# Three reorderings in a fused two-layer transformer trunk: ties on weight splits and residual additions, gate and up products grouped by half, and a split last output tile

## The chip, the cores and the metric

The kernel runs on one core of one Trainium2 chip. The metric is the device time of one execution in microseconds (us), lower is better. TensorE (PE; its weight loads are PEld) multiplies, VectorE (DVE) and ScalarE (ACT) do the elementwise work, GpSimd (POOL) a few small operations, and the queue of SyncE (SP) issues nearly all transfers.

## The reference

A trunk of two pre-norm layers on a residual stream x of 256 tokens by 1024 features, in float32:

```
for layer in (0, 1):
    h = rmsnorm(x, norm_mix[layer])
    x = x + mixer[layer](h @ w_in) @ w_out        # even: indexed sparse + differential attention; odd: compressed + selected + window attention
    h = rmsnorm(x, norm_ffn[layer])
    x = x + (silu(h @ w_gate) * (h @ w_up)) @ w_down      # 2816 hidden features
return rmsnorm(x, norm_final)
```

## The kernel before, in words

Tokens lie in two tiles t = 0, 1 of 128. Every float32 product of an activation with a weight is made of three in a reduced format: each operand is split into a high part (a rounding copy on ACT) and a low part (the difference, on DVE), and high x high, high x low and low x high are added up in PSUM. In the gate and up products (L438, L439) the activation's high and low parts lie side by side, so that one product of 512 columns takes both against the weight's high part, and a second of 256 columns adds the weight's low part.

Weights stream through the class `Weights` as 200 tiles of up to 128 x 1024, in the order of use: per layer the input projection, eight tiles of the output projection, 44 of gate and up, 22 of the down projection. `load` issues a transfer on SP's queue (four raw buffers), `prepare` makes the high part (L110, ACT) and the low part (L113, DVE; seven buffers of each), and `next` hands a tile out and prepares up to six ahead. With `hold=tail` the last tiles of an output or down projection are handed out together.

`residual` multiplies out a projection for the four quarters (t, h), h being a half of 512 features. It runs k by k over all quarters, and for the last `tail` k quarter by quarter, so that one quarter ends early: its sum is added to x (L382 or L384) and the next norm's work on it begins (`Norm.half`: weighting by the gain, four transposes, the split into `aW`; or `Final.half` for the output). In the mixers the order is (0,0), the first half of (0,1), (1,0), the rest of (0,1), (1,1). `amid` is called after the first entry; in the even mixer it transposes and splits the attention output of tile 1.

The softmax of the odd mixer (`softmax_terms`, L401 on DVE and L402 on ACT) runs for two groups gp, each for t = 0, 1; then the terms are scaled (L917, DVE), transposed (L922), copied out (L218) and multiplied by the values (L938).

The program is written in order, but a planner lists each engine's instructions: among those that are ready by its own clock it takes the one of the highest priority, which follows program order. A NoSync tie fixes only the order of two instructions in the list of one engine; `keep_in_program_order` (`pin`) ties an instruction behind all that was traced before it on its engine. Each engine then works through its list in order.

Of the kernel before, what the change touches and what calls it, by code (L numbers as in the profile page):

```python
# [55 lines left out]
C_SEL = C_CMP + NT * 16  # L56
C_BM = C_SEL + 2 * P
C_KM = C_BM + 8
C_END = C_KM + 2

# [14 lines left out]
class Weights:  # L75


    def __init__(self, tc, pool, rpool, flats, specs, ahead, bufs, spare):
# [9 lines left out]
        self.ready = []  # L88
        self.used = 0

# [7 lines left out]
    def prepare(self, upto, behind=False):  # L98

        nc = self.tc.nc  # L100
        while len(self.ready) < min(upto, len(self.queue)):
# [8 lines left out]
            act = nc.scalar.activation(hi[:, :n], raw[:, :n], AF.Copy)  # L110
            if behind:
                self.tc.keep_in_program_order(act)
            nc.vector.tensor_sub(lo[:, :n], raw[:, :n], hi[:, :n])  # L113
# [11 lines left out]
def trunk(tc, x, w0, w1, sm0, cw, vec, gcol, cst, out, dbg=None):  # L125
# [91 lines left out]
    def evac(dst, src):  # L217
        A.activation(dst, src, AF.Copy)  # L218
# [21 lines left out]

    def split(hi, lo, src):
        A.activation(hi, src, AF.Copy)
        V.tensor_sub(lo, src, hi)  # L243

    def split_T(dst, k0, src, n, behind=False):

        pt = t_bank("pt_a").rearrange("p (k c) -> p k c", k=4)
        for i in range(n):
            mmi = TE.transpose(pt[:, i], src[:, i * P : (i + 1) * P], ident)
            if behind:  # L250
                pin(mmi)
        split(dst[0][:, k0 : k0 + n], dst[1][:, k0 : k0 + n], pt[:, :n])

    class Norm:


        def __init__(self, goff):
            self.goff = goff
            self.wide, self.aT = new_wide()
            self.rs = [small_tile(1, "rs") for _ in range(NT)]  # L260
            self.last = None
            self.ms = [None] * NT

        def finish(self):

            if self.last is not None:
                split_T(self.aT[NT - 1], 4, self.last, 4, behind=True)
                self.last = None

        def half(self, t, h):  # L270
# [5 lines left out]
            else:  # L276
                split_T(self.aT[t], 4 * h, xg, 4)
# [28 lines left out]
    class Final:  # L306


        def __init__(self):
            self.ms = [small_tile(2, "ms2") for _ in range(NT)]  # L310
            self.y = [[nat("y") for _ in range(2)] for _ in range(NT)]

        def half(self, t, h):
            ms = self.ms[t]
            c = slice(512 * h, 512 * h + 512)
            sq = ap.tile([P, 512], BF16, tag="sq", bufs=2, name="sq")
            A.activation(sq, xs[t][:, c], AF.Square, scale=1.0 / math.sqrt(D), accum_out=ms[:, h : h + 1])
            V.tensor_mul(self.y[t][h], xs[t][:, c], gains[V_FIN][:, c])
            if h == 1:
                rf = small_tile(1, "ms")  # L320
                rsqrt_sum(rf, ms)
                for h in range(2):
                    c = slice(512 * h, 512 * h + 512)
                    y = self.y[t][h]
                    if h == 0:
                        A.activation(y, y, AF.Copy, scale=rf)
                    else:
                        V.tensor_scalar(y, y, rf, None, op0=ALU.mult)
                    (A, nc.sync)[h].dma_start(out[t * P : (t + 1) * P, c], y)

    def mm3(ps, act, k, wh, wl, start, stop):
        TE.matmul(ps, act[0][:, k], wh, start=start, stop=False)  # L332
        TE.matmul(ps, act[0][:, k], wl, start=False, stop=False)  # L333
        TE.matmul(ps, act[1][:, k], wh, start=False, stop=stop)  # L334
# [15 lines left out]
    def residual(act, nk, tail, nxt, rs=None, amid=None):  # L350

        ps = [[mm_bank("ps_out") for _ in range(2)] for _ in range(NT)]

        def one(t, h, k, wt):
            c = slice(512 * h, 512 * h + 512)
            mm3(ps[t][h], act[t], k, wt[0][:, 0, c], wt[1][:, 0, c], k == 0, k == nk - 1)
# [7 lines left out]
        if amid:  # L364
# [5 lines left out]
        for t, h, k0, k1 in order:  # L370
            c = slice(512 * h, 512 * h + 512)
            for k in range(k0, k1):
                one(t, h, nk - tail + k, last[k])
# [7 lines left out]
            if rs is None:  # L381
                V.tensor_add(xs[t][:, c], ps[t][h], xs[t][:, c])  # L382
# [706 lines left out]
```

## Time and profile before

| what | value |
|---|---|
| time, median of 3 runs | 656.94 us (656.31 to 657.65) |
| the profiled execution | 658.92 us, of which the span of its trace is 657.1 us |
| PE / DVE / ACT / POOL busy | 98% / 74% / 60% / 2% of the span |
| granted clock of PE | full speed (2.4 GHz level) nearly throughout; mean 0.997 |
| read from HBM | 107.46 MB, 165 GB/s over the span |

Starts and durations in the rows below are us from the start of the span, means are ns. Matmuls overlap and their ends are modelled: the pace is read from start to start. "[0.70 <-DVE xg L273]" is idle time of the engine just before the instruction, and what ended it.

The stages by time: even mixer to 138, its gate and up to 263, down projection to 325, odd mixer to 467, its gate and up to 590, down projection to 650, then the end of the final norm and the store.

### The profile page before, as it was taken

Reading aid. Unit: us, or ns where it says so; the run is one execution under the profiler, and the core shown is the slowest. Engines: PE = TensorE matmul, PEld = TensorE weight load, DVE = VectorE, ACT = ScalarE, POOL = GpSimd, SP = SyncE. Lnnn points to the kernel's source line nnn. Section 1 sums busy time; section 2 is a strip of 40 time slices with the busy share of each in tenths; the row PEclk is TensorE's granted clock in tenths of the full one; section 3 lists DMA queues with packets and bytes.
Section 4 is the critical chain, followed back from the end, with each engine's and each line's share of the span. In section 5 each row is a group of like instructions: output and inputs, shape, how many; then the busy total and the mean of one; then the engine's idle time right before and its main releaser. Section 6 shows DMA issues by size and latency. Waiting matters only on the chain.

```text
span 657.1 us, 10010 instructions
## 1 busy us (share of the span) xinstructions
PE 643.1 (98%) x3512; PEld 537.5 (82%) x3512; DVE 489.0 (74%) x1115; ACT 395.7 (60%) x800; POOL 12.9 (2%) x26
## 2 busy tenths in 40 slices
PE   8999999999999999999999999999999999999995
PEld 5979888788888888888887877776888888888884
DVE  6999977778877777544588888796788787875424
ACT  6686758557655555433476698696586555554312
POOL 2000000000000000000000000000000000000000
PEclk9999999999999999999999999999999999999998
DMA  8834354418765665664187331412176555555501
GB/s 309 305 118 145 97 189 134 126 35 290 237 182 188 192 185 181 190 196 143 49 342 268 105 95 64 161 33 97 67 262 247 189 188 192 182 191 192 193 23 65
DMA packets 31729, 109.15 MB, mean 166 GB/s; under 512 B 3648, under 2 KB 3904, under 8 KB 31424
## 3 DMA queue, kind: packets, MB, share of 16 engines
q1 hardware_dynamic: 31104, 107.92, 49.2%
q10 hardware_dynamic: 576, 0.59, 0.3%
q8 instruction: 28, 0.46, 0.3%
q14 instruction: 21, 0.17, 0.1%
HBM read 107.46 MB, written 1.05 MB: 165 GB/s over the span
## 4 chain that ended last, share of the span: by engine, by line
PE 84%; DVE 8%; ACT 3%; issue 2%; DMA 1%; POOL 0%; SPq 0%; POOLq 0%; DVEq 0%; ACTq 0%
PE ps_g L438 12%; PE ps_u L438 12%; PE ps_out L332 7%; PE ps_out L334 7%; PE ps_out L333 7%; PE ps_g L439 6%; PE ps_u L439 6%; PE ps_in L333 4%; PE ps_in L332 4%; PE ps_in L334 4%; DVE w_lo L113 3%; PE ps_o L938 2%; PE ps_s L903 2%; PE pt_p L922 1%; PE ps_s L624 1%
## 5 line engine op out<-in xcount | busy, mean ns | idle before, releaser
L113 DVE TENSOR_TENSOR w_lo<-w_raw,w_hi 128x1024 fp32r<-128x1024 f32 (+5 forms) x200 | 234.7, 1180 | 90.1 <-ACT w_hi L110 87.3
L110 ACT ACTIVATE w_hi<-w_raw 128x1024 fp32r<-128x1024 f32 (+5 forms) x200 | 203.0, 1023 | 127.5 <-PE ps_out L334 56.8
L438 PE MATMUL ps_g<-aW,w_hi 128*128 128x512 f32 x352 | 124.5, 396 | 0.3 <-DVE aW L243 0.3
L438 PE MATMUL ps_u<-aW,w_hi 128*128 128x512 f32 x352 | 124.4, 395 | 0.0
L439 PE MATMUL ps_g<-aW,w_lo 128*128 128x256 f32 x352 | 98.7, 280 | 0.0
L439 PE MATMUL ps_u<-aW,w_lo 128*128 128x256 f32 x352 | 98.7, 280 | 0.0
L438 PEld LDWEIGHTS ps_g<-aW,w_hi 128*128 128x128 f32 x352 | 66.0, 187 | 16.4 <-DVE aW L243 0.9
L438 PEld LDWEIGHTS ps_u<-aW,w_hi 128*128 128x128 f32 x352 | 66.0, 187 | 15.4
L333 PE MATMUL ps_in<-w_lo,aW 128*128 128x512 f32 (+5 forms) x208 | 76.9, 370 | 0.1
L332 PE MATMUL ps_in<-w_hi,aW 128*128 128x512 f32 (+5 forms) x208 | 76.7, 369 | 0.1
L334 PE MATMUL ps_in<-w_hi,aW 128*128 128x512 f32 (+5 forms) x208 | 75.8, 365 | 0.0
L333 PE MATMUL ps_out<-w_lo,hT_hi 128*128 128x512 f32 x176 | 68.6, 390 | 0.0
L334 PE MATMUL ps_out<-w_hi,hT_lo 128*128 128x512 f32 x176 | 68.6, 390 | 0.0
L332 PE MATMUL ps_out<-w_hi,hT_hi 128*128 128x512 f32 x176 | 68.6, 390 | 0.0
L439 PEld LDWEIGHTS ps_g<-aW,w_lo 128*128 128x128 f32 x352 | 66.5, 189 | 0.0
L439 PEld LDWEIGHTS ps_u<-aW,w_lo 128*128 128x128 f32 x352 | 66.5, 189 | 0.0
L333 PEld LDWEIGHTS ps_in<-w_lo,aW 128*128 128x128 f32 x208 | 39.3, 189 | 4.7 <-issue 0.5
L332 PEld LDWEIGHTS ps_in<-w_hi,aW 128*128 128x128 f32 x208 | 39.2, 189 | 4.8 <-ACT w_hi L110 0.3
L334 PEld LDWEIGHTS ps_in<-w_hi,aW 128*128 128x128 f32 x208 | 39.3, 189 | 4.6 <-issue 0.5
L402 ACT ACTIVATE e<-e,bias 128x128 f32<-128x128 f32 (+1 forms) x96 | 42.4, 445 | 0.9 <-DVE bias L401 0.9
L334 PEld LDWEIGHTS ps_out<-w_hi,hT_lo 128*128 128x128 f32 x176 | 33.0, 188 | 6.8
L333 PEld LDWEIGHTS ps_out<-w_lo,hT_hi 128*128 128x128 f32 x176 | 33.0, 188 | 6.8
(225 smaller groups left out, 888.1 us busy)
## 6 DMA issues: line engine op xcount, KB each, us to landing
w_raw<-in_w SPq DMA_DIRECT2D x176, 512.0 KB, 4.3
w_raw<-in_w SPq DMA_DIRECT2D x8, 384.0 KB, 4.6
gain<-in_vec SPq DMA_DIRECT2D x4, 512.0 KB, 5.4
cw<-in_cw SPq DMA_DIRECT2D x2, 1024.0 KB, 8.5
w_raw<-in_w SPq DMA_DIRECT2D x4, 416.0 KB, 5.6
w_raw<-in_w SPq DMA_DIRECT2D x4, 328.0 KB, 5.2
w_raw<-in_w SPq DMA_DIRECT2D x4, 304.0 KB, 2.9
x<-in_x SPq DMA_DIRECT2D x4, 256.0 KB, 5.2
```

The lines of the kernel that those rows point to most:

```text
L110: act = nc.scalar.activation(hi[:, :n], raw[:, :n], AF.Copy)
L113: nc.vector.tensor_sub(lo[:, :n], raw[:, :n], hi[:, :n])
L332: TE.matmul(ps, act[0][:, k], wh, start=start, stop=False)
L333: TE.matmul(ps, act[0][:, k], wl, start=False, stop=False)
L334: TE.matmul(ps, act[1][:, k], wh, start=False, stop=stop)
L402: A.activation(e, e, AF.Exp, scale=-1.0, bias=bias, accum_out=den)
L438: TE.matmul(dst[f], wh[:, i, c], wide[:, k].rearrange("p z q -> p (z q)"), start=k == 0, stop=False)
L439: TE.matmul(dst[f][:, :T], wl[:, i, c], wide[:, k, 0], start=False, stop=k == KD - 1)
L624: TE.matmul(sb[:, i], qT[:96, h0 + i, tq], kT[:96, h0 + i, :ns], start=True, stop=True)
L903: mmi = TE.matmul(sb[:, i], qS[t][:, h], kz[:, par, :, :ns], start=z == 0, stop=z == 1)
L922: TE.transpose(pt[:, i, b, st], e[:, i, b, st * P : (st + 1) * P], ident)
L938: pin(TE.matmul(ob[64 * par : 64 * par + 64], vv[:, st, c : c + 64], pTs[par][:, b, st].rearrange("p j c -> p (j c)"), start=False, stop=l ...
```

## The change

The diff, cut to its core. `behind(ins, other)` adds a NoSync tie.

```diff
 Weights.prepare:
+            with self.tc.high_priority(offset=-self.later):
                 act = nc.scalar.activation(hi[:, :n], raw[:, :n], AF.Copy)
...
+                sub = nc.vector.tensor_sub(lo[:, :n], raw[:, :n], hi[:, :n])
+                self.parts.append((act, sub))
 Final:
+        def square(self, t, o, n, last=False):
+            i = self.part[t]
+            self.part[t] += 1
+            ms, total = self.ms[t], self.sum[t]
+            sq = ap.tile([P, 512], BF16, tag="sq", bufs=2, name="sq")
+            pin(A.activation(sq[:, :n], xs[t][:, o : o + n], AF.Square, scale=1.0 / math.sqrt(D), accum_out=ms[:, i : i + 1]))
+            if not last:
+                pin(A.activation(total, ms[:, i : i + 1], AF.Identity, bias=total))
+                if t == 0:
+                    A.activation(small_tile(1, "warm"), total, AF.Sqrt)
+            if last:
+                self.rf = small_tile(1, "ms")
+                A.activation(self.rf, ms[:, i : i + 1], AF.Sqrt, bias=total)
+        def weigh(self, t, h):
+            c = slice(512 * h, 512 * h + 512)
+            V.tensor_mul(self.y[t][h], xs[t][:, c], gains[V_FIN][:, c])
+        def end(self, t):
+            rf = self.rf
+            V.reciprocal(rf, rf)
...
-                rsqrt_sum(rf, ms)
 residual:
-            order = [(0, 0, 0, tail), (0, 1, 0, tail // 2), (1, 0, 0, tail), (0, 1, tail // 2, tail), (1, 1, 0, tail)]
+        if amid and not hold:
+            order = [(t, h, 0, tail) for t, h in ((0, 0), (0, 1), (1, 0), (1, 1))]
+        elif amid:
+            order = [(0, 0, 0, tail), (0, 1, 0, tail // 2), (1, 0, 0, tail), (0, 1, tail // 2, tail), (1, 1, 0, tail)]
...
+            if isinstance(nxt, Final) and (t, h) == (NT - 1, 1):
+                px = t_bank("ps_x")
+                for q, (dst, o, n) in enumerate(((ps[t][h], 0, 256), (px, 256, 256))):
+                    cq = slice(c.start + o, c.start + o + n)
+                    for k in range(tail):
+                        wt = last[k]
+                        mm3(dst[:, :n], act[t], nk - tail + k, wt[0][:, 0, cq], wt[1][:, 0, cq], q == 1 and k == 0, k == tail - 1, q == 0)
+                    cx = cq if q else c
+                    V.scalar_tensor_tensor(xs[t][:, cx], dst[:, : cx.stop - cx.start], rs[t], xs[t][:, cx], op0=ALU.mult, op1=ALU.add)
+                    nxt.square(t, cq.start, n, q == 1)
+                nxt.weigh(t, h)
+                nxt.end(t)
+                continue
             for k in range(k0, k1):
-                one(t, h, nk - tail + k, last[k])
+                made = one(t, h, nk - tail + k, last[k])
+                if hold and k0:
+                    for mmi in made:
+                        behind(mmi, column)
+                if inorder and (t, h, k) == (1, 0, 0):
+                    for mmi in nxt.turned[0, 0]:
+                        behind(mmi, made[-1])
+            if (t, h) == (1, 0):
+                column = made[-1]
+                if inorder:
+                    for mmi in nxt.turned[0, 1]:
+                        behind(mmi, column)
...
+                if gate:
+                    behind(add, gate[0])
 ffn:
                     for g in range(KD // kk):
-                        wh, wl = W.next()
-                        for i in range(kk):
-                            k = g * kk + i
-                            for f in range(nf):
...
+                        wt = W.next()
+                        todo += [(wt, i, g * kk + i, f) for i in range(kk) for f in range(nf)]
+                        if f0 and g < KD // kk - 1:
+                            continue
+                        for wt, i, k, f in todo:
+                            TE.matmul(dst[f], wt[0][:, i, f * P : (f + 1) * P], wide[:, k].rearrange("p z q -> p (z q)"), start=k == 0, stop=False)
+                        for wt, i, k, f in todo:
+                            TE.matmul(dst[f][:, :T], wt[1][:, i, f * P : (f + 1) * P], wide[:, k, 0], start=False, stop=k == KD - 1)
 even_mixer:
+            residual(oT, KD, 4, nxt, amid=lambda: parts.extend(split_T(oT[1], 4, ods[1], 4, pinned=True)[1]))
+            for i in (8, 9):
+                behind(W.parts[o0 + i][1], mixed)
+            behind(nxt.added, parts[1])
+            for part, ins in zip(W.parts[o0 + 10], parts):
+                behind(part, ins)
 odd_mixer:
+            residual(oT, KD, 4, nxt, amid=lambda: None, gate=(scaled, copied), hold=True)
+            for i, first in ((5, (1, 0)), (6, (1, 0)), (7, (1, 1))):
+                for part, term in zip(W.parts[o0 + i], reversed(begun[first])):
+                    behind(term, part)
+            for i in (8, 9):
+                for part, ins in zip(W.parts[o0 + i], (copied, scaled)):
+                    behind(part, ins)
 trunk:
+    W.later = 100
     n = odd_mixer(n, V_FFN1)
+    W.later = 0
```

`o0` is the number of the first tile of the mixer's output projection, so tiles o0+8, 9 and 10 are the first three of gate and up. `mixed` is the last combination of the two softmax maps in the even mixer (L690); `scaled` and `copied` are the odd mixer's last L917 and the last copy of transposed terms (L218); `begun[gp, t]` is the first pair of `softmax_terms`; `nxt.added` is the addition of quarter (0,0); `nxt.turned[t, h]` are a quarter's transposes. The first chunk of gate and up (f0 = 0) keeps high and low alternating within each weight tile. `later` lowers the priority of the odd mixer's splits by 100 places. The constants lose two unused parts, 258 of 938 columns of their larger transfer.

## Rows read from the trace of the kernel before

**Rows 1.** The page: busy time, share of the span and instructions of each engine.

```profile
PE 643.1 (98%) x3512; PEld 537.5 (82%) x3512; DVE 489.0 (74%) x1115; ACT 395.7 (60%) x800; POOL 12.9 (2%) x26
```

**Rows 2.** The waits of PE in the whole span: who is waited for, us in total, times, longest. The two shown are the longest within the kernel's work.

```profile
PE pt_p L922 <- DVE e L917: 1.4, 2, 1.1
...
PE pt_x L294 <- DMA x<-in_x: 1.1, 1, 1.1
```

**Rows 3.** Four stretches of PE work without a pause: the even layer's gate and up, the odd layer's, the even layer's down projection (512 columns each), one projection of the odd mixer of 256 columns each. Columns: stretch and its length, busy us and instructions of PE, PEld, DVE, ACT, POOL, granted clock, DMA share, GB/s. Each stretch begins and ends at the start of a product; PE's count takes in the one to three that still run at its edges.

```profile
159.35:215.88 56.53, 56.53 (x322) 49.00 (x321) 45.60 (x74) 33.20 (x61) 0.00 (x0) 1.00 0.66 210
485.72:541.19 55.47, 55.47 (x321) 48.91 (x320) 45.32 (x74) 33.33 (x62) 0.00 (x0) 1.00 0.61 214
274.94:304.86 29.92, 29.92 (x133) 24.77 (x132) 13.48 (x11) 11.66 (x11) 0.00 (x0) 1.00 0.59 181
333.06:337.73 4.67, 4.67 (x42) 4.67 (x40) 4.38 (x12) 1.99 (x3) 0.00 (x0) 1.00 0.98 351
```

**Rows 4.** The timeline of PE at the end of the even mixer: start, duration, instruction.

```profile
120.39 0.39 PE L333 MATMUL ps_out<-w_lo,aT 128*128 128x512 f32 x1
121.01 0.44 PE L608 MATMUL pt_p<-con,pd 128*128 128x128 f32 x2 [0.24 <-DVE pd L690]
...
128.84 0.39 PE L333 MATMUL ps_out<-w_lo,aT 128*128 128x512 f32 x1
129.92 0.66 PE L249 MATMUL pt_a<-con,xg 128*128 128x128 f32 x4 [0.70 <-DVE xg L273]
```

**Rows 5.** The timeline of DVE in the same stretch.

```profile
119.10 1.21 DVE L113 TENSOR_TENSOR w_lo<-w_raw,w_hi 128x1024 fp32r<-128x1024 f32 x1
...
127.32 1.22 DVE L113 TENSOR_TENSOR w_lo<-w_raw,w_hi 128x1024 fp32r<-128x1024 f32 x1
128.46 0.69 DVE L382 TENSOR_TENSOR x<-ps_out,x 128x512 f32<-128x512 f32 x1
129.18 0.69 DVE L273 TENSOR_TENSOR xg<-x,gain 128x512 f32<-128x512 f32 x1
129.79 0.68 DVE L243 TENSOR_TENSOR aT<-pt_a,aT 128x512 fp32r<-128x512 f32 x1
```

**Rows 6.** The timeline of DVE at the end of the odd mixer.

```profile
433.85 0.42 DVE L401 CUSTOM_DVE_ANT_0 e<-ps_s,con 128x256 f32<-128x256 f32 x1
...
439.49 1.22 DVE L113 TENSOR_TENSOR w_lo<-w_raw,w_hi 128x1024 fp32r<-128x1024 f32 x1
...
449.36 1.22 DVE L113 TENSOR_TENSOR w_lo<-w_raw,w_hi 128x1024 fp32r<-128x1024 f32 x1
...
450.58 0.67 DVE L382 TENSOR_TENSOR x<-ps_out,x 128x512 f32<-128x512 f32 x1
...
451.31 0.67 DVE L273 TENSOR_TENSOR xg<-x,gain 128x512 f32<-128x512 f32 x1
...
452.49 1.22 DVE L113 TENSOR_TENSOR w_lo<-w_raw,w_hi 128x1024 fp32r<-128x1024 f32 x1
453.63 0.61 DVE L917 TENSOR_SCALAR e<-e,den 128x256 f32<-128x256 f32 x2
```

**Rows 7.** The timeline of PE in the same stretch, and (last line) the group of one kind of product between 459.95 and 467.05.

```profile
451.75 0.39 PE L334 MATMUL ps_out<-w_hi,aT 128*128 128x512 f32 x1
452.39 0.63 PE L922 MATMUL pt_p<-con,e 128*128 128x128 f32 x4 [0.25 <-DVE e L917]
454.12 0.41 PE L922 MATMUL pt_p<-con,e 128*128 128x128 f32 x2 [1.10 <-DVE e L917]
...
467.10 0.50 PE L438 MATMUL ps_g<-aW,w_hi 128*128 128x512 f32 x1 [0.28 <-DVE aW L243]
...
L332 PE MATMUL ps_out<-w_hi,aT 128*128 128x512 f32 x8 | 3.3, 414 | 0.1
```

**Rows 8.** The timeline of all engines at the end of the kernel.

```profile
649.01 0.74 DVE L384 SCALAR_TENSOR_TENSOR x<-ps_out,rs,x 128x512 f32<-128x512 f32 x1
...
649.84 0.39 PE L334 MATMUL ps_out<-w_hi,hT_lo 128*128 128x512 f32 x1
650.40 0.74 DVE L384 SCALAR_TENSOR_TENSOR x<-ps_out,rs,x 128x512 f32<-128x512 f32 x1
651.17 0.63 ACT L317 ACTIVATE sq<-x 128x512 bf16<-128x512 f32 x1 [0.66 <-DVE x L384]
651.71 0.19 ACT L317 ACTIVATION_READ_ACCUMULATOR sq<-x 128x1 f32 x1
...
652.22 0.55 POOL L227 TENSOR_TENSOR ms<-ms,half 128x1 f32<-128x1 f32 x1 [3.65 <-DVE ms L226]
652.80 0.72 ACT L326 ACTIVATE y<-y,ms 128x512 f32<-128x512 f32 x1 [0.91 <-POOL ms L227]
```

**Rows 9.** Groups of one shape (by line, engine and form: count, busy us, mean ns): small and half-width forms, and table loads.

```profile
L394 DVE SCALAR_TENSOR_TENSOR rope_b<-ps_in,rs,con 128x256 f32<-128x256 f32 x16 | 7.1, 474 | 0.0
L912 DVE RECIPROCAL den<-den 128x2 f32<-128x2 f32 x16 | 2.5, 158 | 0.5 <-ACT e L402 0.5
L242 ACT ACTIVATE hT_hi<-hn 128x256 fp32r<-128x256 f32 x44 | 17.9, 409 | 0.9 <-DVE hn L452 0.7
L449 ACT ACT_TABLE_LOAD x2 | 2.6, 1283 | 0.0
```

**Rows 10.** Issues of transfers: count, KB each, us from issue to landing.

```profile
con<-in_cst SPq DMA_DIRECT2D x1, 469.0 KB, 6.5
```

More of the change, by code (lines that the diff above doesn't have):

```diff
@@ L88, in __init__ @@
         self.ready = []
+        self.parts = []
         self.used = 0
+        self.later = 0
     def load(self, upto):
@@ L261, in __init__ @@
             self.last = None
+            self.turned = {}
             self.ms = [None] * NT
@@ L266, in finish @@
             if self.last is not None:
-                split_T(self.aT[NT - 1], 4, self.last, 4, behind=True)
+                split_T(self.aT[NT - 1], 4, self.last, 4, pinned=True)
                 self.last = None
@@ L309, in __init__ @@
         def __init__(self):
-            self.ms = [small_tile(2, "ms2") for _ in range(NT)]
+            self.ms = [small_tile(3, "ms3") for _ in range(NT)]
+            self.sum = [small_tile(1, "msum") for _ in range(NT)]
             self.y = [[nat("y") for _ in range(2)] for _ in range(NT)]
-        def half(self, t, h):
[L314 to L318, printed above, removed]
-            if h == 1:
-                rf = small_tile(1, "ms")
-                rsqrt_sum(rf, ms)
[L322 to L334, printed above, removed]
+            self.part = [0] * NT
+            for total in self.sum:
+                G.memset(total, EPS)
+        def square(self, t, o, n, last=False):
[11 more added lines that the diff above has]
+                A.activation(self.rf, ms[:, i : i + 1], AF.Sqrt, bias=total)
@@ new lines, in weigh @@
+        def weigh(self, t, h):
[4 more added lines that the diff above has]
+            V.reciprocal(rf, rf)
+            for h in range(2):
+                c = slice(512 * h, 512 * h + 512)
+                y = self.y[t][h]
+                if h == 0:
+                    A.activation(y, y, AF.Copy, scale=rf)
+                else:
+                    V.tensor_scalar(y, y, rf, None, op0=ALU.mult)
+                (A, nc.sync)[h].dma_start(out[t * P : (t + 1) * P, c], y)
@@ new lines, in half, with mm3 @@
+        def half(self, t, h):
+            self.square(t, 512 * h, 512, h == 1)
+            self.weigh(t, h)
+            if h == 1:
+                self.end(t)
+    def mm3(ps, act, k, wh, wl, start, stop, skip=False):
+        return (
+            TE.matmul(ps, act[0][:, k], wh, start=start, stop=False, skip_group_check=skip),
+            TE.matmul(ps, act[0][:, k], wl, start=False, stop=False, skip_group_check=skip),
+            TE.matmul(ps, act[1][:, k], wh, start=False, stop=stop, skip_group_check=skip),
+        )
@@ L712, in even_mixer @@
             nxt = Norm(goff)
-            residual(oT, KD, 4, nxt, amid=lambda: split_T(oT[1], 4, ods[1], 4, behind=True))
+            o0 = W.used
+            parts = []
+            residual(oT, KD, 4, nxt, amid=lambda: parts.extend(split_T(oT[1], 4, ods[1], 4, pinned=True)[1]))
[4 more added lines that the diff above has]
+                behind(part, ins)
         return nxt
```

73 lines of the change are left out of this document (36 added, 37 removed).

## The prediction

> **What bounds the kernel now.** I read the page first: PE is busy 98% of the span, DVE 74%, ACT 60% [rows 1]. Busy here is a union of overlapping products, so the reader has to see two other things: where PE pauses, and at what pace it runs when it does not. The view of waits gives the pauses. They are few: the longest is 1.4 us in two pieces on the scaled softmax terms of the odd mixer, then 1.1 us on the first transfer of x at the start [rows 2]. A pause of less than the overlap of two products does not show there, so the timelines of PE are read from start to start. The pace comes from four stretches without a pause [rows 3]. A down projection starts 132 products of 512 columns in 29.92 us, 226.7 ns each. A projection of 256 columns starts 39 in 4.67 us, 119.7 ns each. In gate and up 160 pairs (one product of 512, one of 256) take 55.47 us in the odd layer, 346.7 ns a pair, which is the sum of the two paces (346.4). In the even layer the same 160 pairs take 56.53 us, 353.3 ns. The granted clock is 1.00 of the 2.4 GHz level in all four, so the 6.6 ns are not the clock: alternating long and short products has two rhythms here, and the even layer runs in the worse one.
>
> So the kernel is bound by PE's stream. An edit pays if it takes away a pause of PE, if it changes a rhythm, or if it shortens the chain after the last product.
>
> **The change part by part.** The sum is made against the profiled execution, 658.92 us with a span of 657.1; the median of the runs is 1.98 us lower, and I carry the difference over unchanged.
>
> *Constants.* 258 columns of 128 x 4 bytes, 129 of 469 KB [rows 10], leave a transfer that the fifth weight tile follows. At 351 GB/s, the highest rate in [rows 3], that is 0.37 us. Most of it lies behind PE work that is not yet fed by those tiles. I take 0.2 us; the bounds are 0 and 0.4.
>
> *End of the even mixer.* PE loses time at two places. The transposes at 121.01 start 0.62 us after the product before them, where 0.23 is the pace: 0.39 us lost [rows 4]. They wait for the combined maps, and DVE made a weight's low part of 1.21 us just before [rows 5]. The tie puts the low parts of tiles o0+8 and o0+9 behind that combination, so this loss goes. The transposes at 129.92 start 1.08 us after the product before them, 0.85 lost [rows 4]. They wait for the weighting at 129.18, which stands behind a low part (127.32) and the addition (128.46) [rows 5]. Now tile o0+10's low part and the addition both stand behind the attention output's own low part (129.79 before, some 1.1 us earlier now), and the transposes stand behind the first three products of (1,0). The addition then ends near 130.1 and the weighting near 130.8, while PE has all twelve products of (0,1) and three of (1,0), 15 x 0.227 = 3.4 us from 127.8, to 131.2. That covers it by 0.4 us. Queued behind the added tie on DVE are the weighting and the transposes of (0,0) alone. The split tiles are needed at 138, when gate and up begin. Sum: 1.24 us lost before; I take 1.2. Bounds: 1.4, and nothing, if another chain moves into the place.
>
> *Gate and up.* No product is added or removed. In ten of eleven chunks of each layer sixteen high products run in a row, then sixteen low ones: 20 groups a layer. At the uniform paces a group takes 16 x 346.4 = 5.54 us. The even layer's groups take 16 x 353.3 = 5.65 us, so 20 x 0.11 = 2.1 us are to be had there, and nothing in the odd layer. What the trace does not show is what changing from 256 to 512 columns costs once per group. From below it is nothing. From above I use the worse rhythm's own excess: if the disturbance lasts three pairs, 3 x 6.6 = 20 ns a group, over 40 groups 0.8 us. I take this upper value, so the gain is 1.3 us. Outer bounds: 2.1 gained; 2.1 lost, if both layers fall into a rhythm as bad as that of the even layer. Each group needs its second high part 0.9 us earlier, and holds the first low part longer; both are covered, since PE has no wait for a weight in either stage and the tiles are prepared several ahead.
>
> *End of the odd mixer.* The last scalings end near 454.2 [rows 6]. On DVE between 449.36 and 453.63 stand two low parts of 1.22 us, the addition of (0,0) and its weighting, 0.67 each [rows 6]. PE loses 0.41 us before the transposes at 452.39 (0.64 instead of 0.23 from 451.75) and 1.1 us before 454.12 [rows 7]. The ties put tiles o0+8 and o0+9 behind the last scaling and the last copy, the four additions behind the last scaling, and tile o0+7, whose low part was made at 439.49, ahead of the first terms of t = 1 at 433.85 [rows 6]. The DVE stretch shortens by the addition, the weighting and one low part, 2.6 us, and by a second one if o0+10 stays behind too; tile o0+7 lengthens an earlier, full stretch by 1.2. Net: scalings 1.4 to 2.6 us earlier. But PE also gets there earlier: between 459.95 and 467.05 run eight products of each of three kinds, 24 in all, which are the twelve of (1,0) and the twelve of (1,1) [rows 7]. The second half of (0,1), six products or 1.36 us, had been used up as filler before 452; it is now held until (1,0) is through. So of the 1.5 us lost here 0.3 to 1.5 remain, while the held products cover what follows (1,0): the 0.28 us before 467.10 and about 0.3 us around the last transposes. I take 1.4 us off; bounds 2.1 and 0. Moved with the splits are two loads on SP's queue, which wait for the raw buffers that the low parts free. They are issued some 3 us later, for tiles that PE reaches after two groups of gate and up, 467.1 + 2 x 5.5 = 478, over 20 us on. POOL's work is not passed by any of it. The lower priority of the other splits I cost at nothing: they are prepared up to six tiles ahead. If that cover is gone, one low part on the path costs 1.22 us.
>
> *The end.* Nine products of 512 columns become eighteen of 256: 18 x 0.120 - 9 x 0.227 = +0.12 us. After the last product (649.84) the chain is an addition of 0.74, a square with its accumulator of 0.73 (651.17 to 651.90), then 0.90 us through DVE and POOL's power to 652.80 [rows 8]. At half width the addition takes 0.47 and the square 0.41 plus 0.10 [rows 9]: -0.27 and -0.22. The power's stretch becomes a square root on one column, for which the accumulator's read is the nearest row, 0.19 [rows 8], or up to 0.3 with its bias as an operand (estimate), a reciprocal of 0.16 [rows 9] and two hand-overs: 0.4 to 0.5, so -0.45. Together -0.8. But DVE is late there: from 649.01 it adds (1,0) and weights it, to about 650.4 [rows 8], and now a 512-wide addition of 0.74 for the first 256 columns stands ahead of the last one. That puts the last addition's end at 651.6, not 650.95, and leaves 0.15 of the gain. Between 0.15 and 0.8 I take 0.4.
>
> A table load takes 1.283 us, and Silu's line has just one in each layer, though copies and splits run on ACT between its 44 uses [rows 9]. The change asks for the new function once early, after the first quarter, where the load lies under PE's last products, so I cost it at nothing. The Trainium skill ("ScalarE: Activation LUTs", What ACT_TABLE_LOAD costs) gives 2.66 us for each switch to another set, with the drain; its section on table sets says that cheap functions stand in every set, and the single load for each layer's Silu agrees.
>
> *Sum:* 0.2 + 1.2 + 1.3 + 1.4 + 0.4 = 4.5 us off 658.92, 654.4 for the profiled execution; on the median, 656.94 - 4.5 = 652.4 us.
>
> **The rivals.**
> *Gate and up buy nothing.* The rhythm depends on what went before, not on the order. For it: both layers run the same instructions and differ. Against it: uniform runs show one pace. Time: 652.4 + 1.3 = 653.7.
> *The odd mixer's wait moves.* The six held products leave PE dry exactly while DVE is still scaling, as computed above at the lower bound, and the cover after (1,0) only pays that back: 652.4 + 1.4 = 653.8.
> *The table is loaded on the last path,* before the last square root, because the squares after the early one want another set. The price is one load of 1.28 us in the chain after the last product: 653.7. By the Trainium skill's 2.66 us for a switch (same page and section) it would be 655.1. Silu's single load in each layer speaks against it.
> *Slower: the tie holds back the softmax instead of pulling the split forward.* The splits of the odd mixer are 100 places lower in priority, and the first terms of t = 1 may not start before tile o0+7 is split. If the planner leaves that split where it is, the terms slip from 433.85 to 440.7, 6.9 us [rows 6], and PE, whose filler already ran out at 452, waits as long. With 3.1 us gained elsewhere that is 656.94 - 3.1 + 6.9 = 660.7. It decides the sign from a slip of 3.1 us on. Against it: tiles are prepared up to six ahead, so the split can be made long before the terms are due.
> *It does not do what it says.* The ties fix orders in the lists, but the planner's clock is not the chip's, and as many new pauses appear as go: only the end and half of the rhythm remain, 656.94 - 1.1 = 655.8.
>
> **How the numbers follow.** The forecast, 652.4, has a chance of 0.55, with its own range 650.3 to 653.6. The rivals: gate and up nothing 0.14, the moved wait 0.12, the table 0.04, slower 0.07, no effect 0.08. A measurement of this kernel can tell about 0.2%, 1.3 us, from no change: faster is below 655.6, slower above 658.3. Faster is 0.55 + 0.14 + 0.12 + 0.04 = 0.85, same 0.08, slower 0.07. For eight in ten the range must leave out the slower case and most of the no-effect case: up to 655.4. Down it goes to 649.8: the upper bounds of all parts (0.4 + 1.4 + 2.1 + 2.1 + 0.8 = 6.8) give 650.1, and a little is left for the odd mixer's other pauses.
>
> **What would show it right or wrong.** Gate and up: in both layers 5.54 to 5.57 us for a group of 32. Even mixer: no idle time of PE before L608 and L249. Odd mixer: the low parts of o0+8 and o0+9 behind the last L917, and idle time before L922 under 1.5 us in all. End: one table load near 646, and about 2.2 us instead of 2.6 from the last product's end to the scaling of y. The prediction is wrong if an odd-mixer stage grows by more than 3 us, if a second table load appears after 648, or if groups of low products run slower than 120 ns each.

## The result, and the profile after

The changed kernel takes 652.27 us, the median of six executions (651.78 to 652.52). The kernel before took 657.33 beside it (six, 656.31 to 660.36): a ratio of 0.9915, 95% interval 0.9895 to 0.9936. Repeated later, it was 652.66 beside 659.38 us, 0.9894 (0.988 to 0.9908). So it is faster, by 0.6 to 1.2%, and the forecast of 652.4 lies within 0.3 us of both medians. The parts of the sum are another matter.

Below, two profiles of each kernel, the second ones from the experiments. A stage is the distance between the first starts of its products and the next stage's in the timeline of PE.

| stage, us | before | before again | after | after again |
|---|---|---|---|---|
| start to the even output projection | 105.04 | 105.05 | 104.98 | 105.00 |
| to gate and up | 33.59 | 33.58 | 32.84 | 32.85 |
| gate and up, even | 125.42 | 123.15 | 123.53 | 123.54 |
| down, even | 61.28 | 61.32 | 61.32 | 61.28 |
| odd mixer | 141.77 | 143.49 | 137.24 | 137.25 |
| gate and up, odd | 123.08 | 123.08 | 123.43 | 123.45 |
| down, odd, to the last product's start | 59.65 | 59.65 | 59.86 | 59.86 |
| from there to the end | 7.29 | 7.28 | 7.21 | 7.21 |

The busy line of the page of the changed kernel, against [rows 1]:

```profile
PE 638.9 (98%) x3521; PEld 537.5 (83%) x3521; DVE 478.9 (74%) x1116; ACT 403.0 (62%) x809; POOL 11.0 (2%) x26
```

It says as little as before: the same shares of a shorter span.

Gate and up, 320 products of each layer as in [rows 3] (columns as there):

```profile
161.15:216.81 55.66, 55.66 (x322) 49.20 (x321) 41.52 (x73) 34.76 (x63) 0.00 (x0) 1.00 0.64 210
483.13:538.80 55.67, 55.67 (x323) 49.19 (x321) 41.42 (x73) 35.47 (x63) 0.00 (x0) 1.00 0.62 214
```

Both layers now take the same, 5.567 us a group of 32, where one had 5.65 and the other 5.547.

PE at the end of the even mixer, against [rows 4]:

```profile
119.45 0.39 PE L363 MATMUL ps_out<-w_hi,aT 128*128 128x512 f32 x1
119.95 0.83 PE L675 MATMUL pt_p<-con,pd 128*128 128x128 f32 x4
...
131.60 0.39 PE L364 MATMUL ps_out<-w_lo,aT 128*128 128x512 f32 x1
131.83 0.66 PE L254 MATMUL pt_a<-con,xg 128*128 128x128 f32 x4
```

The transposes of the weighting (L254) follow 0.23 us after a product: that wait is gone. Those of the maps (L675) still start 0.50 after theirs. They come 1.06 us earlier than before, but the product ahead of them comes 0.94 earlier too, so of the 0.39 us lost there 0.27 remain.

DVE and then PE at the end of the odd mixer, against [rows 6, 7]:

```profile
445.19 0.62 DVE L993 TENSOR_SCALAR e<-e,den 128x256 f32<-128x256 f32 x2
445.72 0.68 DVE L442 TENSOR_TENSOR x<-ps_out,x 128x512 f32<-128x512 f32 x1
...
447.93 3.50 DVE L114 TENSOR_TENSOR w_lo<-w_raw,w_hi 128x1024 fp32r<-128x1024 f32 x3 [0.80 <-ACT w_hi L111]
```

```profile
445.39 0.40 PE L365 MATMUL ps_out<-w_hi,aT 128*128 128x512 f32 x1
445.69 0.63 PE L998 MATMUL pt_p<-con,e 128*128 128x128 f32 x4
```

Three low parts and the addition now stand behind the last scalings, and the last transposes of terms follow a product without idle time: both pieces of the 1.4 us of [rows 2] are gone.

The end, all engines, against [rows 8]:

```profile
639.13 1.28 ACT L334 ACT_TABLE_LOAD   x1
...
642.21 0.72 ACT L350 ACTIVATE y<-y,ms 128x512 f32<-128x512 f32 x1 [0.64 <-DVE ms L345]
...
643.19 0.28 PE L365 MATMUL ps_x<-w_hi,hT_lo 128*128 128x256 f32 x1
...
643.37 0.63 ACT L330 ACTIVATE sq<-x 128x512 bf16<-128x512 f32 x1 [0.44 <-ACT y L350]
...
644.00 0.48 DVE L416 SCALAR_TENSOR_TENSOR x<-ps_x,rs,x 128x256 f32<-128x256 f32 x1
...
645.05 0.40 ACT L330 ACTIVATE sq<-x 128x256 bf16<-128x256 f32 x1
...
646.10 0.72 ACT L350 ACTIVATE y<-y,ms 128x512 f32<-128x512 f32 x1 [0.23 <-DVE ms L345]
```

From the last product's start to the scaling of y it takes 2.91 us, 2.96 before. The last addition ends at 644.48, but the last square waits for ACT until 645.05.

### The profile page after: what moved, and what is told of

Its sections match the earlier page's. It is cut to its first block, busy times and chain, and to the rows that moved or that the text cites. A ratio compares the mean times of both kernels' runs of the same rounds, so it can differ in the third digit from the quotient of the medians.

```text
span 650.4 us, 10025 instructions
## 1 busy us (share of the span) xinstructions
PE 638.9 (98%) x3521; PEld 537.5 (83%) x3521; DVE 478.9 (74%) x1116; ACT 403.0 (62%) x809; POOL 11.0 (2%) x26
## 3 DMA queue, kind: packets, MB, share of 16 engines
HBM read 107.32 MB, written 1.05 MB: 167 GB/s over the span
## 4 chain that ended last, share of the span: by engine, by line
PE 88%; ACT 4%; DVE 4%; DMA 2%; issue 1%; SPq 0%; POOL 0%; ACTq 0%; DVEq 0%
PE ps_g L503 12%; PE ps_u L503 12%; PE ps_out L364 8%; PE ps_out L365 8%; PE ps_out L363 8%; PE ps_u L505 6%; PE ps_g L505 6%; PE ps_in L364 5%; PE ps_in L365 5%; PE ps_in L363 5%; PE pt_p L998 2%; PE ps_o L1014 2%; PE ps_s L978 1%; DVE w_lo L114 1%; ACT e L466 1%
## 5 line engine op out<-in xcount | busy, mean ns | idle before, releaser
L503 PE MATMUL ps_u<-aW,w_hi 128*128 128x512 f32 x352 | 84.9, 391 | 0.0
L503 PE MATMUL ps_g<-aW,w_hi 128*128 128x512 f32 x352 | 84.5, 391 | 0.0
L364 PE MATMUL ps_out<-w_lo,hT_hi 128*128 128x512 f32 (+1 forms) x176 | 68.3, 388 | 0.0
L363 PE MATMUL ps_out<-w_hi,hT_hi 128*128 128x512 f32 (+1 forms) x176 | 68.3, 388 | 0.0
L365 PE MATMUL ps_out<-w_hi,hT_lo 128*128 128x512 f32 (+1 forms) x176 | 68.3, 388 | 0.0
L505 PEld LDWEIGHTS ps_u<-aW,w_lo 128*128 128x128 f32 x352 | 45.4, 191 | 1.9
L505 PEld LDWEIGHTS ps_g<-aW,w_lo 128*128 128x128 f32 x352 | 45.4, 191 | 1.9
L505 PE MATMUL ps_g<-aW,w_lo 128*128 128x256 f32 x352 | 46.0, 283 | 0.0
L505 PE MATMUL ps_u<-aW,w_lo 128*128 128x256 f32 x352 | 46.0, 283 | 0.0
L363 PEld LDWEIGHTS ps_out<-w_hi,hT_hi 128*128 128x128 f32 x176 | 33.1, 188 | 6.7
```

The costliest lines, as they stand in the source:

```text
L363: TE.matmul(ps, act[0][:, k], wh, start=start, stop=False, skip_group_check=skip),
L364: TE.matmul(ps, act[0][:, k], wl, start=False, stop=False, skip_group_check=skip),
L365: TE.matmul(ps, act[1][:, k], wh, start=False, stop=stop, skip_group_check=skip),
L503: TE.matmul(dst[f], wt[0][:, i, f * P : (f + 1) * P], wide[:, k].rearrange("p z q -> p (z q)"), start=k == 0, stop=False)
L505: TE.matmul(dst[f][:, :T], wt[1][:, i, f * P : (f + 1) * P], wide[:, k, 0], start=False, stop=k == KD - 1)
```

## The experiments

**The kernel before, once more.** No edit.

> The kernel before, unchanged, profiled once more. Its first profiled execution took 658.92 us, 2 us over the median of its runs, and lost 1.9 us in the odd mixer's products with the values (L938: 12.84 us for 48 starts, against 10.99 in the changed kernel), where a weight's high part on ACT stands ahead of the copy that the second product of a pair waits for. Theory (the order of ACT's list does this, so it is there in every execution): again 12.5 to 12.9 us for L938, the odd mixer from the first projection to the first gate product at 141 to 142 us. Rival (that execution was an unlucky one): L938 near 11.0 and the odd mixer 2 us shorter. In both, the even layer's gate and up groups at 5.65 us if the rhythm belongs to the program, 5.55 if it changes from execution to execution.

659.48 us (beside 659.17; ratio 0.9996, 0.9982 to 1.0009). The table shows that neither the even gate and up nor the odd mixer repeats: the first is 2.3 us shorter, the second 1.7 us longer, together 0.5 us less. Gate and up:

```profile
161.93:217.40 55.47, 55.47 (x322) 48.91 (x321) 44.79 (x74) 33.52 (x63) 0.00 (x0) 1.00 0.69 213
489.83:545.30 55.47, 55.47 (x322) 48.91 (x321) 44.15 (x71) 33.38 (x63) 0.00 (x0) 1.00 0.64 210
```

The same program now runs its even layer in the better rhythm. The rhythm belongs to the execution, not to the layer. In the odd mixer the products with the values took 14.58 us, each counted from its start to the next start on PE (12.84 in the first profile), so neither theory nor rival has the number. The wait, then ACT, then PE in that place:

```profile
PE ps_o L938 <- ACT pT L218: 1.5, 1, 1.5
```

```profile
412.91 1.06 ACT L110 ACTIVATE w_hi<-w_raw 128x1024 fp32r<-128x1024 f32 x1 [3.64 <-DMA w_raw<-in_w]
413.87 0.58 ACT L218 ACTIVATE pT<-pt_p 128x512 f32<-128x512 f32 x1
```

```profile
411.98 1.07 PE L938 MATMUL ps_o<-pT,vv 128*64 128x512 f32 x2
414.50 3.65 PE L938 MATMUL ps_o<-pT,vv 128*64 128x512 f32 x14 [1.46 <-ACT pT L218]
```

A weight's high part waits 3.64 us for its transfer at the head of ACT's list. Behind it stands the copy that the next product with the values needs. That order is in the list and so in every execution (in the first profile too the same high part stands ahead of the same copy, at 413.41 and 414.37); how much it costs depends on when the transfer lands. The first product that needs the copy started 2.53 us after the first of its sixteen here, and 0.79 us in the first profile.

**Without the lower priority.**

```diff
-    W.later = 100
+    W.later = 0
```

> The changed kernel with the odd mixer's splits at their old priority (later = 0); all ties stay. My prediction cost this lowering at nothing. Theory from the two traces: it is what puts the copies of the transposed terms ahead of the weights' high parts on ACT, so without it the products with the values take 12.8 us instead of 11.0 and the odd mixer 1.5 to 2.5 us more: 654 to 655 us. Rival (the ties do it all, the priority nothing): within 0.4 us of the changed kernel, 651.9 to 652.7, products with the values at 11.0.

655.88 us beside 659.17 (0.9943, 0.9924 to 0.9962), more than the theory's 654 to 655. The odd mixer took 140.63 us, 3.4 more than in the changed kernel; 1.6 of it are the products with the values (12.62 against 10.99), 0.8 the scores, and the rest pieces of 0.1 to 0.4 us on transposes and other products. ACT and PE at one stage of sixteen such products, in this run and then in the changed kernel:

```profile
411.03 1.06 ACT L111 ACTIVATE w_hi<-w_raw 128x1024 fp32r<-128x1024 f32 x1 [1.75 <-DMA w_raw<-in_w]
411.99 0.58 ACT L220 ACTIVATE pT<-pt_p 128x512 f32<-128x512 f32 x1
...
411.98 4.29 PE L1014 MATMUL ps_o<-pT,vv 128*64 128x512 f32 x16
416.20 0.66 PE L906 MATMUL pt_q<-con,stk 128*128 128x128 f32 x4
```

```profile
406.59 0.60 ACT L220 ACTIVATE pT<-pt_p 128x512 f32<-128x512 f32 x1 [1.70 <-PE pt_p L998]
407.09 1.05 ACT L111 ACTIVATE w_hi<-w_raw 128x1024 fp32r<-128x1024 f32 x1
...
407.38 3.65 PE L1014 MATMUL ps_o<-pT,vv 128*64 128x512 f32 x16
410.96 0.44 PE L906 MATMUL pt_q<-con,stk 128*128 128x128 f32 x2
```

With the old priority the weight's high part goes first and the copy ends after the products have begun; the stage takes 4.22 us instead of 3.58. For the 1.8 us outside these products the cause was not traced. The priority, which I had cost at nothing, is the largest single part.

**Without the odd mixer's ties.**

```diff
-            residual(oT, KD, 4, nxt, amid=lambda: None, gate=(scaled, copied), hold=True)
-            for i, first in ((5, (1, 0)), (6, (1, 0)), (7, (1, 1))):
...
-            for i in (8, 9):
...
+            residual(oT, KD, 4, nxt, amid=lambda: None, odd=True)
```

`odd` only keeps the odd mixer's order of quarters, which `hold` had told apart.

> The changed kernel without the odd mixer's ties: no order of terms, splits and additions, the second half of (0,1) not held; the lowered priority stays. Theory (the ties clear DVE before the last scalings, as in my prediction, 1.4 us, and the priority did the rest of the 4.5 us): the odd mixer takes 138.3 to 138.9 us instead of 137.2, and the wait before the last transposes of terms (L998) is back with 0.8 to 1.5 us: 653.4 to 654.0 us. Rival (once the splits give way, the ties have nothing left to do): 137.2 us, the same time as the changed kernel.

654.39 us beside 659.38 (0.9919, 0.9906 to 0.9931); 652.66 for the changed kernel in the same comparison. The odd mixer took 139.11 us, 1.9 more. The waits of PE there:

```profile
PE pt_p L998 <- ACT pT L220: 0.8, 1, 0.8
PE pt_p L998 <- DVE e L993: 0.3, 1, 0.3
PE ps_g L503 <- DVE aW L247: 0.3, 1, 0.3
```

The rival falls: with the splits out of the way, two additions and a weighting still stand among the last scalings on DVE, and the 0.3 us before the first gate product is back. DVE:

```profile
445.93 0.67 DVE L442 TENSOR_TENSOR x<-ps_out,x 128x512 f32<-128x512 f32 x1
...
446.63 0.69 DVE L281 TENSOR_TENSOR xg<-x,gain 128x512 f32<-128x512 f32 x1
447.24 0.61 DVE L993 TENSOR_SCALAR e<-e,den 128x256 f32<-128x256 f32 x2
...
447.84 0.67 DVE L442 TENSOR_TENSOR x<-ps_out,x 128x512 f32<-128x512 f32 x1
```

**The kernel before with the lower priority alone.** The edit is `W.later = 100` around `odd_mixer`, and the priority in `prepare`.

> The kernel before with nothing but the lowered priority of the odd mixer's splits. Theory (the copies of the transposed terms stand behind weights' high parts on ACT; taken alone, the lowering gives what the changed kernel without the ties has, 139.1 us for the odd mixer): 2.5 to 4.3 us off the 141.8 and 143.5 of the kernel before, so 655 to 656.5 us where the kernel before has 659.2. Rival (it pays only together with the ties): the odd mixer at 141 us or more.

656.98 us beside 658.63 (0.9969, 0.9955 to 0.9983), executions from 653.41 to 657.56. The odd mixer took 139.11 us in the profile, as without the ties: 2.7 or 4.4 us less than in the two profiles of before. The profiled execution was the fastest of the twelve, 653.41, and had both gate and up stages in the better rhythm; the wide spread of the others was not traced. So the stage took what the theory said, but the median gained 1.65 us and lies outside its 655 to 656.5.

With this run the odd mixer has been measured all four ways: 141.77 and 143.49 us with neither the ties nor the lowering, 140.63 with the ties alone, 139.11 with the lowering alone, 137.24 with both. The lowering is worth 2.7 to 4.4 us alone and 3.4 with the ties, the ties 1.1 to 2.9 alone and 1.9 with the lowering.

**Gate and up in pairs again.** In `ffn` the inner loop of the kernel before is put back.

> The changed kernel with the old order in gate and up: one high product, one low product, alternating. Theory (alternation falls into the worse rhythm in the even layer because of how this program arrives there, runs of sixteen cannot): even layer's groups of 32 back at 5.65 us, odd layer's at 5.547, so +1.9 and -0.35: 653.8 us. Rival (which rhythm a layer gets is decided by small shifts, and the even mixer's end has shifted): one of even 5.55 and odd 5.547, 651.2 us, faster than the change, or both layers at 5.65, 656.0 us.

654.23 us beside 659.17 (0.9923, 0.9902 to 0.9943), 653.61 to 656.61.

```profile
161.75:217.22 55.47, 55.47 (x322) 48.50 (x321) 44.80 (x74) 33.53 (x63) 0.00 (x0) 1.00 0.70 213
483.86:540.39 56.53, 56.53 (x323) 49.05 (x321) 44.84 (x74) 33.57 (x63) 0.00 (x0) 1.00 0.63 208
```

Now it is the odd layer that runs in the worse rhythm, and the even one in the better: neither theory's numbers, but the rival's mechanism. From start to start the worse rhythm repeats every three pairs: in the first profile of before 232, 241 and 235 ns for the long product, 118, 120 and 114 for the short one, against 230 and 117 in every pair of the better there. In the better layer of this run the starts vary a little from pair to pair (231 to 233 and 112 to 118), with the same sum. Of eight alternating layers traced here two were in the worse.

**Runs of eight.**

```diff
-                        if f0 and g < KD // kk - 1:
+                        if f0 and g < 0:
```

> The changed kernel with gate and up in runs of eight high and eight low products, twice as many changes between 256 and 512 columns. Theory (a change costs 20 ns, as 5.567 us a group of 32 against 5.547 for the sum of the two paces says): 5.587 us for 32 products in both layers, 0.4 us a layer more: 653.1 to 653.4 us. Rival (the 20 ns belong to long runs of low products, which start 120 ns apart, and not to the change): 5.55 to 5.567 us.

652.81 us beside 658.63 (0.9909, 0.9891 to 0.9928).

```profile
161.46:217.32 55.86, 55.86 (x322) 49.15 (x321) 42.89 (x75) 34.03 (x63) 0.00 (x0) 1.00 0.69 212
484.12:539.98 55.86, 55.86 (x322) 49.16 (x321) 42.85 (x75) 34.29 (x63) 0.00 (x0) 1.00 0.64 217
```

5.587 us for 32 products in both stretches: twice the changes, twice the 20 ns, as the theory had it. PE's starts show where they lie, here and in the runs of sixteen alike: after a change to 512 columns the first five products start some 233, 236, 228, 233 and 231 ns apart where the later ones keep 227, and after the change back the first takes 113 or 114 instead of 120.

**Without the even mixer's part.** The ties behind `mixed` and `parts` go, and the old order of quarters comes back.

> The changed kernel without the even mixer's ties and with its old order of quarters. My prediction gave this part 1.2 us; between the traces the stage from the first output product to the first gate product went from 33.59 to 32.84 us. Theory (the wait on the weighting of (0,0) goes, a part of it comes back at the end of the stage): 33.6 us again, 0.75 us slower than the changed kernel. Rival (the full 1.2 us is there and something else costs 0.4): 34.0 us or more.

653.93 us beside 659.38 (0.9907, 0.9893 to 0.9922). The stage to gate and up took 33.62 us, 0.77 more. The waits of PE there:

```profile
PE pt_a L254 <- DVE xg L281: 0.7, 1, 0.7
PE pt_p L673 <- DVE pd L755: 0.2, 1, 0.2
```

The part is worth 0.77 us in its stage. The median is 1.27 us above the changed kernel's 652.66, half a microsecond more; the profiled execution, 2.04 us above the changed kernel's, took 0.57 more up to the first output product and 0.59 more in the odd mixer, which was not followed up.

**The even mixer's splits lowered too.** `W.later = 100` also around `even_mixer`.

> The changed kernel with the splits of the even mixer lowered by 100 places too. Theory (in the odd mixer the lowering pays because copies to be multiplied next stand behind splits; the even mixer's waits in the trace are small, 0.6 us in all after its start): a gain of 0 to 0.5 us in the stretch to the first gate product, 137.3 to 137.8 us. Rival (there the splits are what PE waits for, so lowering them starves the projections): the stretch grows by 1 us or more.

654.98 us beside 659.38 (0.9928, 0.9915 to 0.9941), 2.3 us above the changed kernel's 652.66, and 3.0 us more up to the first output product (108.00 against 105.00). New waits of PE in its first 60 us:

```profile
PE ps_i L616 <- ACT iT L220: 0.7, 1, 0.7
PE pt_i L577 <- DVE n L574: 0.6, 1, 0.6
PE ps_v L643 <- ACT kT L220: 0.3, 1, 0.3
```

Theory wrong. The rival's cost is there, but the longest waits are not for weights: they are for copies and normed rows. One of 0.2 us there is for a weight's low part. All waits shown there make up 2.0 us, against 0.8 in the changed kernel, so most of the 3.0 us has no cause shown. The lowering is no rule.

**The old end.** `Final`, the last quarter and its products as before.

> The changed kernel with the final norm and the last quarter as before: one product width of 512, one addition, the power on POOL. My prediction gave the new end 0.4 us. Theory from the trace: nothing is left of it, since ACT is now late: the last square waits 0.57 us behind the squares, reads and sums before it, so 652.1 to 652.4 us, and from the start of the last product to the scaling of y 2.96 us against 2.91. Rival (the prediction's term): 652.7 us or more.

652.51 us beside 659.17 (0.989, 0.9873 to 0.9908). That is just above the theory's 652.1 to 652.4, and not in the rival's range. From the last product's start to the scaling of y 2.96 us, to the end 7.28. The new end is worth nothing.

**The first tile's final scaling on POOL.**

```diff
-                if h == 0:
+                if t == 0:
+                    G.tensor_scalar(y, y, rf, None, op0=ALU.mult)
+                elif h == 0:
...
-                (A, nc.sync)[h].dma_start(out[t * P : (t + 1) * P, c], y)
+                (A if t else nc.sync, nc.sync)[h].dma_start(out[t * P : (t + 1) * P, c], y)
```

> The changed kernel with both scalings of the final norm's first tile (t = 0) on POOL instead of ACT and DVE, and their stores issued by SP. The old end made no difference (652.51 us beside 652.27 and 652.66 for the changed kernel), so the new end earns nothing. Theory: ACT is what is late there; its scaling of t = 0 (0.72 us from 642.21) holds up the square of (1,0), and every square, read and sum after it follows without a pause to 645.05, 0.57 us after the last addition. With that scaling gone the chain to the scaling of y for t = 1 starts 0.4 to 0.6 us earlier: 2.3 to 2.5 us after the start of the last product instead of 2.91. Rival (the additions on DVE set the end): 2.8 to 2.9 us as before.

652.61 us beside 658.63 (0.9912, 0.9895 to 0.9928). PE, ACT and POOL:

```profile
643.42 0.28 PE L367 MATMUL ps_x<-w_hi,hT_lo 128*128 128x256 f32 x1
```

```profile
642.37 0.63 ACT L330 ACTIVATE sq<-x 128x512 bf16<-128x512 f32 x1 [0.57 <-DVE x L450]
642.58 3.91 POOL L350 TENSOR_SCALAR y<-y,ms 128x512 f32<-128x512 f32 x2 [179.81 <-DVE ms L345]
...
645.54 0.72 ACT L352 ACTIVATE y<-y,ms 128x512 f32<-128x512 f32 x1 [0.23 <-DVE ms L345]
```

The square of (1,0) starts as soon as its addition ends, and y is reached after 2.12 us instead of 2.91. This edit takes a scaling from ACT and one from DVE, so it does not single out ACT: the last addition, too, ends 0.89 us after the last product's start instead of 1.29. That ACT is late in the changed kernel is shown by its own trace, where the last square waits 0.57 us for ACT. But POOL needs 1.92 and 2.01 us for the two halves, and the end is 7.43 us after the last product's start, not 7.21.

**One half on POOL.** The same with `(t, h) == (0, 0)`, so that DVE keeps its scaling.

> The changed kernel with only the first half's scaling of t = 0 moved from ACT to POOL, and its store issued by SP. With both halves on POOL, ACT's chain reached the scaling of y for t = 1 2.12 us after the start of the last product instead of 2.91, so ACT was what was late; but POOL took 3.91 us for the two, a store waited for it, and the last product's start to the end stayed at 7.42 us against 7.21. Theory: with one half on POOL, done about 644.4, the store is no longer last and the gain reaches the end: 2.2 to 2.5 us to the scaling of y, 6.6 to 6.8 us to the end, 0.4 to 0.6 us off the changed kernel's 652.3 to 652.7. Rival (the stores' transfers, not the scaling, set the end): 7.1 us or more to the end.

652.05 us beside 658.9 (0.9902, 0.988 to 0.9924): no difference from the changed kernel that can be told. y came after 2.96 us, the end after 7.24. DVE and ACT:

```profile
642.44 0.91 DVE L354 TENSOR_SCALAR y<-y,ms 128x512 f32<-128x512 f32 x1
...
643.28 0.74 DVE L418 SCALAR_TENSOR_TENSOR x<-ps_out,rs,x 128x512 f32<-128x512 f32 x1
...
644.05 0.42 ACT L330 ACTIVATE sq<-x 128x256 bf16<-128x256 f32 x1 [1.17 <-DVE x L418]
```

Here ACT waits for DVE. DVE's scaling of the other half took 0.91 us beside POOL's, where it took 0.48 in the changed kernel, and the additions came that much later. Theory wrong: with ACT alone relieved, DVE is the late one, as my prediction had it. Only the run before, which relieved both, brought y forward.

**The changed kernel, once more.**

> The changed kernel, unchanged, once more, as the measure for the runs beside it. The first two profiles of the kernel before differ: the even layer's gate and up took 5.65 us a group in one and 5.547 in the other, and the odd mixer 141.8 us against 143.5. Theory (runs of sixteen and the lowered priority take away both of these): the changed kernel repeats within 0.2 us in every stage: 5.567 us a group in both layers, the odd mixer 137.2 us. Rival (it varies as the kernel before does): a stage differs by 1 us or more.

652.66 us beside 659.38 (0.9894, 0.988 to 0.9908). Every stage repeats within 0.05 us, as the theory said.

## Why the prediction was right, and where its steps were not

The time came out within 0.3 us, and that closeness is luck. The profiled executions differ by 6.7 us (658.92 and 652.22) where the sum had 4.5. Two errors cancelled: the sum was 2.2 us short, and the 1.98 us between the profiled execution and the median of before, "carried over unchanged", were not there in the changed kernel (652.22 profiled, median 652.27). The kernel before moves by 2 us between comparisons (medians 657.33 to 659.38), so the 4.5 is 0.6 to 2.2 us short on the medians too. What was right is that PE's pauses and pace bound the kernel, and most of the pauses that would go; the sizes were not. Part by part:

- *Constants*, 0.2: the stage before the even output projection is 0.06 us shorter, and varied from 104.6 to 105.6 over executions with the same new constants. Not resolved.
- *End of the even mixer*, 1.2: 0.75 in the traces, 0.77 by taking it out. The step on the weighting held in full. The step "so this loss goes" on the maps failed: DVE combines them 1.05 us earlier, PE arrives 0.94 earlier, and 0.27 of the 0.39 us remain.
- *Gate and up*, 1.3: 1.54 between the first two profiles, 1.89 gained in the even layer and 0.35 lost in the odd one. The cost of 20 ns a group was right, and so was the thought that a change disturbs a few products; that it equals the worse rhythm's excess over three pairs, from which I took it, is a coincidence as far as the runs show (five long products and one or two short ones are disturbed). "The even layer runs in the worse one" was true of one execution. Against the second profile of before this part loses 0.7 us. What it buys is that none of the 18 layers traced with runs of sixteen took more than 123.6 us, where the worse rhythm takes 125.4.
- *End of the odd mixer*, 1.4: 4.5 or 6.2. The ties bring 1.9 by their removal, more than I took, since none of the wait remained before the last transposes of terms: the scalings end 5.8 us earlier from the stage's start, and PE reached them no sooner than they did. The step that failed is "the lower priority of the other splits I cost at nothing": 3.4 us by its removal. I had looked for weights that would come late. What mattered, for 1.6 of the 3.4, was what the splits stood in front of on ACT: the copies of transposed terms. The products with the values use half the array's columns and run two at a time (starts 7 and 423 ns apart in three of the changed kernel's four stages, 0.43 us a pair). A stage grows by about as much as the copy is late: in one stage of sixteen the first product behind the copy starts 0.01 us after the stage's first in the changed kernel, 0.65 without the lowering, 0.79 and 2.53 in the two profiles of before, and the stage takes 3.58, 4.22, 4.37 and 6.10 us. The Trainium skill ("TensorEngine Tiling (Array Packing)", Key Properties) says that tiles of the array work independently of each other, and that a change of tiling drains it. The trace agrees with the first, by the 7 ns between two starts. For the second there are signs only: after the last of these products the next one on the whole array starts 0.52 us later in every stage, where pair follows pair after 0.43; and in the first profile of before a score product stood between two of them, 0.52 us after the one ahead and 0.43 us before the next, where among others of its kind it takes 0.23. No run singles out the drain.
- *The end*, 0.4: nothing. The stage from the last product's start is 0.08 shorter, but that start comes 0.21 later; together 0.12 or so is lost, as much as I took for the eighteen products alone, and nothing of the chain's gain is left. From the last product's end to the scaling of y it took 2.63 us, where I had 2.2 (2.57 before). The step that failed is "DVE is late there": it left out ACT, which is later still, with three squares, three reads and two sums in a row behind the scaling of t = 0; with ACT alone cleared DVE follows closely. That scaling itself waits for DVE's reciprocal at 642.03, which stands behind the addition of (1,0) although its root was ready at 641.57; no run moved it.
- *The table load* came once, at 639.13, and no second followed; the squares after it needed none. That is the 646 of the prediction in a kernel 6.7 us shorter. ACT was idle again for 0.64 us before the scaling at 642.21, so the load cost nothing, and neither the 1.28 us of the row nor the 2.66 of the Trainium skill ("ScalarE: Activation LUTs", What ACT_TABLE_LOAD costs) stood in the chain.

Of the rivals, none came true in its time. The one on the other side, terms held back by the split of o0+7, did not: its low part stands at 424.16, before the terms are due. "Gate and up buy nothing" was right in its reason, that the rhythm depends on what went before, and against the second profile of before in its outcome too. Why an execution falls into one rhythm or the other stays open.

## What to carry to other kernels

Where splits or loads of a stream prepared far ahead share an engine with short copies on the path, give the copies the higher priority, but do it stage by stage: the same line gained 3.4 us in one mixer and lost 2.3 us in all when put on the other too. A profile of one execution shows one rhythm; an order that showed only one in every trace was worth its small fixed cost (652.3 to 652.7 us, against 654.2 with the alternation). Profile the kernel before twice, stage by stage, before giving a part its size. At the end of a kernel, sum the queue of every engine in the last chain, not only of the one that looks late.

## What the hardware showed that was not expected

- Alternating products of 512 and 256 columns settle into one of two rhythms, 346.7 or 353.3 ns a pair, at full clock, in the same program and with no wait in sight. Within a run the starts settle to one pace (227 and 120 ns), and each change of size and back costs 20 ns, spread over the first five long products.
- POOL took 1.91 to 2.01 us for a scaling of 128 x 512 that takes ACT 0.72 and DVE 0.48, and beside it DVE's own took 0.91 in one run. The Trainium skill ("GPSIMD Engine Reference", Specifications) says that the two share their way into SBUF, and that DVE's instructions in a mode with two ports or with two operands in SBUF collide there. The runs don't settle it: with both halves on POOL, DVE's weighting (two such operands, at 644.34) kept its 0.69 us and its scaling (at 645.55) took 0.49, both within POOL's span.
